# The modulation of the MLP half, summed between GLA's tasks in place of beside Hyena

## The chip, the cores and the metric

The program runs on one core of a Trainium2 chip, as one launch. A core has a matrix engine (TensorE, PE, with its weight loads shown as PEld), a vector engine (DVE), a scalar engine (ACT), GpSimd (POOL), a queue that issues most loads (SP) and 16 DMA engines. Each engine takes its instructions strictly in the order in which they were laid down when the program was built, and waits on semaphores for the others. The metric is the device time of an execution in microseconds; shorter is better.

## The reference

Two parts follow one another on one sequence of 1024 tokens of width 1024, with 256 context tokens, all in float32. The change lies in the first part, one block:

```python
silu_c = jax.nn.silu(c)
sh1, sc1, g1, sh2, sc2, g2 = jnp.split((silu_c @ w_mod[l] + b_mod[l])[:, None, :], N_MOD, axis=-1)
h = modulate(x, norm1_g[l], sh1, sc1)
...
y, yc = mixer(h, hc, rows, with_ctx_out, w_in[l], w_out[l], ...)   # [Hyena | GLA | GatedDeltaNet] @ w_out
x = x + g1 * y
x = x + g2 * sq_relu_mlp(modulate(x, norm2_g[l], sh2, sc2), w_mlp1[l], w_mlp2[l])
```

Of the six vectors of modulation, g1 is needed at the out-projection, sc2 and sh2 behind it, and g2 at the end of the MLP. Each is a row of 1024 numbers: the product of a vector of 1024 with a 1024 x 1024 part of w_mod. The second part, two layers of windowed attention and mLSTM, is not touched.

## The kernel before

The code emits instructions in the order of the Python program; a static scheduler then lays down the order of each engine by dependencies, buffers and its own estimates of durations. A buffer is a tile of a pool under a tag; a tag with two buffers lets two tiles take turns, and a load into a third waits until the last reader of the first is done. Matrix products in float32 are made of three products of high and low halves, so a weight tile is loaded raw, and split into hi (ACT) and lo (DVE or POOL).

Block 1 runs: modulation of the mixers' half, norm, in-projection, preparation of GDN (the gated delta net), then the scan of GDN in two lanes of two heads each, ten steps a head, then Hyena (two long convolutions by hand-written Fourier matrices, hy_mix and hy_conv), then GLA (gla_mix), then the out-projection (out_rows), and the MLP. The scheduler lets the scan run beside Hyena and GLA. The scan loads each head's k and q (L1275, L1276) and makes W in L1323.

The MLP half's four vectors come from mods1 (L1565), one block each in the order g1, sc2, sh2, g2. A block, mod_block (L371), has eight pieces: a load of 128 x 1024 of w_mod on SP into tile mr (L375, 512 KB, tag "wr" of two buffers), a scaling by the vector's entries on ACT (in place; the first piece writes the accumulator ma, tag "wh" of two buffers), and for the other seven a sum into ma on POOL (L387). Then eight matmuls with a column of ones sum ma over partitions, and DVE adds the bias. For g1 and g2 col_row turns the columns into a row in memory, by way of a small tile crow and a DMA on POOL's queue. That makes 32 loads, 32 scalings and 28 sums.

GLA goes through two head pairs p, each of two groups of tokens with levels of 64, 32, 16, 8, 4, 2, 1 and 0 tokens and an output; its products of decays with q and k are on POOL (eq and ek in L873, L874, and in L909 for the outputs), the exponentials on ACT, the differences on DVE (L867 to L870). A hook, step(p, i), is called between its tasks, 20 times for each p. At p = 1, i = 8 it loads g1 as a broadcast row and emits the eight tiles of w_out (wo_tile, L1556): a load into tag "wr", a multiplication by g1 on POOL (L1561), then hi and lo. At i = 12 and 14 the first half of GLA's rows is normalized. The results of the mixers go through memory, tensor yT, from which the out-projection loads tiles, also in tag "wr" (L1533), and splits them into ch (ACT) and cl (POOL).

PSUM has eight banks. The scan keeps three, mods1 has a pool of one and Hyena one of four.

Of the kernel before, what the change touches and what calls it, by code (L numbers as in the profile page):

```python
# [9 lines left out]
F32 = mybir.dt.float32  # L10
# [9 lines left out]
D = 1024  # L20
# [146 lines left out]
class Builder:  # L167
# [226 lines left out]
            nc.vector.tensor_add(out=outs[v], in0=p[:, v * 8 : v * 8 + 8], in1=b)  # L394
        yield

    def col_row(self, name, col):

        p = self.ps()
        self.tp(p[:8, :128], col)  # L400
        t = self.small([8, 128], "crow", 2)
        self.nc.vector.tensor_copy(out=t, in_=p[:8, :128])
        row = self.dram(name, [1, D])
        self.nc.gpsimd.dma_start(out=row[0].rearrange("(j p) -> j p", p=128), in_=t)
        return row
# [1156 lines left out]
        self.split(raw, hi, lo, leng=leng)  # L1562
        return hi, lo

    def mods1(self, tl):  # L1565

        A, c = self.A, self.sc["cc"][:, :, 0]
        m = {}
        for j, nm in ((2, "g1"), (4, "sc2"), (3, "sh2"), (5, "g2")):
            t = self.const(nm, [128, 8])  # L1570
            for _ in self.mod_block(tl, A["w_mod"][0][:, j * D : j * D + D], self.c["b_mod"][:, j * 8 : j * 8 + 8], [c], [t], "pool"):
                pass
            m[nm] = self.col_row(nm + "row", t) if nm[0] == "g" else t
        m["gs2"] = self.gs_cols("gs2", m["sc2"], self.c["norm2_g"])
        return m

    def mods2(self, tl, md):

# [130 lines left out]
    def block1(self, x3, ey):  # L1709
# [16 lines left out]
        with ExitStack() as e1:  # L1726
# [9 lines left out]
            with ExitStack() as e2:  # L1736
# [13 lines left out]
                tl = lambda tag, bufs, shape=(128, TT), dt=F32: self.tiler(pools[tag])(tag, bufs, shape, dt)  # L1750
# [34 lines left out]
            egg.close()  # L1785
            with ExitStack() as es:
                ep = ExitStack()
                ep.enter_context(self.psums(px=1))
                pmod = self.pools
                ep.enter_context(self.psums(px=4))  # L1790
                with ExitStack() as eh:
                    hl = self.tiler(self.pool(eh, "hym"))
                    ml = lambda tag, bufs, shape: self.wp.tile(list(shape), F32, name=self.nm(tag), tag={"mr": "wr", "ma0": "wh"}[tag], bufs=2)
                    eh.enter_context(self.smalls())
                    self.hy_mix(F, dr["hy"], yT, hl)
                    pmix, self.pools = self.pools, pmod
                    m = self.mods1(ml)
                    self.pools = pmix
                ep.close()
                es.enter_context(self.psums(pq=2, px=3))  # L1800

                eq, eA, eB = (ExitStack() for _ in range(3))
                with right():
                    eq.enter_context(self.psums(pm=3))
                    pm = self.pools["pm"]
                    eB.enter_context(self.smalls())
                    ol, lB, lA = (self.tiler(self.pool(e, n)) for e, n in ((eB, "o1"), (eB, "o1b"), (eA, "o1a")))
                wo = {}
                rows = lambda u, t: u[t * 128 : t * 128 + 128, :]
                KO = (0, 1, 5, 6, 7, 2, 3, 4)  # L1810
                hn = [None, None]
                op = self.pool(es, "orl")
                orows = op.tile([128, 8, 384], F32, name="orowsl")
                norm = lambda g: self.head_norm_out(orows, self.c["gla_ng"], dr["gla_gate"], yT, 256, self.tiler(op), self.ps, (g,))

                def step(p, i):
                    if p == 1:
                        if i == 8:
                            g1 = self.row_bc(self.wp.tile([128, D], F32, name="g1", tag="wh", bufs=2), m["g1"])
                            for k in KO:  # L1820
                                wo[k] = self.wo_tile(lA if k in (0, 1, 5, 6, 7) else lB, self.A["w_out"][0], k, gate=g1)
                        if i == 12:
                            hn[0] = norm(0)
                            next(hn[0])
                        if i == 14:
                            for _ in hn[0]:
                                pass

                with self.smalls():
                    self.gla_mix(sub("gla_"), orows, step)  # L1830
                hn[1] = norm(1)
                for _ in hn[1]:
                    pass
# [642 lines left out]
```

## Time and profile before

| | |
|---|---|
| median of three runs | 3687.88 us (3683.22 to 3688.8) |
| profiled execution | 3682.15 us |
| its span | 3680.4 us |
| PE, DVE, ACT, POOL busy | 3336.0, 2266.0, 1523.4, 1331.9 us |

The profile is of one execution. Busy time is the sum of an engine's instructions; the time of the profiled execution has 1.75 us around the span. Stretches are named by their time from the start of the span: GDN's preparation ends and Hyena's first convolution runs at about 758 to 841 us, Hyena ends at about 929, GLA's first pair runs from about 960 to 1073 and its second to about 1199, where the main block of the out-projection starts.

### The profile page before, as it was taken

The page shows a single profiled execution, that of the slowest core. Times are in us where ns is not written, and L with a number is a line of the kernel's source. Part 1 is how long each engine was busy: PE and PEld are TensorE (multiplying, and loading weights), DVE is VectorE, ACT ScalarE, POOL GpSimd, SP SyncE. Part 2 cuts the span into 40 slices and gives each one's busy share as a digit, 9 for nine tenths or more (in the row PEclk, how much of TensorE's full clock was granted, in tenths as well). Part 3 has the DMA queues.
Part 4 walks back from the last instruction along what each step waited for, and adds up shares of the span by engine and source line. Part 5 has one row for each costly group of instructions (what it writes and reads, how often), then busy time and mean ns, then how long its engine had stood idle before and what let it go on. Part 6 is the DMA issues. An engine that isn't in the chain of part 4 may idle for free.

```text
span 3680.4 us, 53188 instructions
## 1 busy us (share of the span) xinstructions
PE 3336.0 (91%) x19802; PEld 2775.0 (75%) x19802; DVE 2266.0 (62%) x4418; ACT 1523.4 (41%) x2967; POOL 1331.9 (36%) x1162
## 2 busy tenths in 40 slices
PE   7999989768896999999999699998899999998997
PEld 5668867656775778877788588887788778876885
DVE  8783642467568365555544756665677757665776
ACT  4443345431333442222211544443565554444662
POOL 2343432564547243333412201112545501113554
PEclk9899988777655999999999899999999999998998
DMA  5433543563313352222221211112544511124444
GB/s 201 145 118 100 142 130 107 192 203 114 94 46 101 121 183 92 74 72 74 90 81 46 70 50 52 51 51 87 152 121 126 170 57 55 55 70 130 121 132 140
DMA packets 346222, 388.03 MB, mean 105 GB/s; under 512 B 58099, under 2 KB 282787, under 8 KB 345964
## 3 DMA queue, kind: packets, MB, share of 16 engines
q1 hardware_dynamic: 322380, 300.33, 27.8%
q0 software_dynamic: 23584, 84.31, 6.3%
q8 instruction: 157, 2.57, 0.3%
q14 instruction: 101, 0.83, 0.1%
HBM read 296.07 MB, written 88.49 MB: 104 GB/s over the span
## 4 chain that ended last, share of the span: by engine, by line
PE 60%; DVE 15%; issue 7%; DMA 6%; ACT 5%; POOL 4%; SPq 1%; POOLq 0%; ACTq 0%; DVEq 0%
PE pm L256 34%; PE px L256 20%; PE pa L256 2%; PE px L265 2%; PE po L256 1%; DVE ma L271 1%; PE pa L265 1%; DMA mr<-in_w_ada 1%; DMA mr<-in_w_mod 1%; DVE ac L271 1%; POOL ma L387 1%; ACT e L268 1%; ACT mr L268 1%; DVE e L287 1%; DVE x L287 1%
## 5 line engine op out<-in xcount | busy, mean ns | idle before, releaser
L256 PE MATMUL pm<-x,wh 128*128 128x512 f32 (+3 forms) x4768 | 1430.2, 381 | 1.8 <-DVE x L287 1.8
L256 PEld LDWEIGHTS pm<-x,wh 128*128 128x128 f32 (+2 forms) x4768 | 863.9, 189 | 165.1 <-issue 8.4
L256 PE MATMUL pm<-x,wl 128*128 128x512 f32 (+3 forms) x2384 | 908.5, 381 | 26.5 <-ACT u L268 19.1
L256 PEld LDWEIGHTS pm<-x,wl 128*128 128x128 f32 (+2 forms) x2384 | 450.3, 189 | 110.6 <-ACT u L268 20.3
L256 PE MATMUL pm<-wo,ch 128*128 128x512 f32 x832 | 271.0, 407 | 0.0
L287 DVE TENSOR_TENSOR wl<-wr,wh 128x1024 fp32r<-128x1024 f32 (+1 forms) x110 | 144.0, 1309 | 170.2 <-ACT wh L268 169.8
L1652 DVE TENSOR_TENSOR oa<-px,oa 128x512 f32<-128x512 f32 x240 | 162.1, 688 | 132.2 <-PE px L256 131.9
L387 POOL TENSOR_TENSOR ma<-ma,mr 128x1024 f32<-128x1024 f32 x63 | 157.3, 2497 | 171.8 <-ACT mr L268 138.0
L268 ACT ACTIVATE u<-pm 128x512 f32<-128x512 f32 (+2 forms) x204 | 108.7, 544 | 261.3 <-PE pm L256 228.1
L256 PE MATMUL px<-w2h,ml 128*128 128x512 f32 x480 | 194.8, 406 | 19.8 <-DVE ml L287 10.1
L256 PE MATMUL px<-w2h,mh 128*128 128x512 f32 x480 | 192.3, 401 | 0.0
L256 PE MATMUL px<-w2l,mh 128*128 128x512 f32 x480 | 191.9, 400 | 0.0
L256 PEld LDWEIGHTS pm<-wo,ch 128*128 128x128 f32 x832 | 161.9, 196 | 32.8
L256 PE MATMUL pm<-wo,cl 128*128 128x512 f32 x416 | 171.1, 411 | 12.8 <-POOL cl L287 9.7
L275 POOL TENSOR_SCALAR mkw<-kr,gws 128x128 f32<-128x128 f32 x144 | 77.7, 543 | 282.0 <-PE px L256 240.2
L268 ACT ACTIVATE wh<-wr 128x1024 fp32r<-128x1024 f32 (+2 forms) x138 | 143.3, 1038 | 27.2 <-PE pm L256 15.4
L2360 DVE TENSOR_REDUCE amx<-pa 128x1 f32<-128x640 f32 (+2 forms) x144 | 107.3, 745 | 73.9 <-PE pa L256 72.8
L268 ACT ACTIVATE e<-e 128x1280 f32<-128x1280 f32 (+3 forms) x126 | 134.0, 1066 | 42.2 <-DVE e L275 38.7
L268 ACT ACTIVATE P<-pa,amx 128x640 f32<-128x640 f32 (+2 forms) x144 | 105.6, 733 | 95.3 <-DVE amx L275 83.9
L268 ACT ACTIVATE w2h<-wr 128x1024 fp32r<-128x1024 f32 x32 | 33.9, 1059 | 265.3 <-PE px L256 226.2
L268 ACT ACTIVATE mr<-mr,silu_cc 128x1024 f32<-128x1024 f32 x63 | 72.3, 1149 | 141.0 <-DVE ma L271 92.0
L1550 POOL TENSOR_TENSOR xr<-or,xr 128x512 f32<-128x512 f32 x72 | 93.3, 1296 | 98.0 <-DVE or L1549 80.9
(895 smaller groups left out, 7137.6 us busy)
## 6 DMA issues: line engine op xcount, KB each, us to landing
wr<-in_w_in SPq DMA_DIRECT2D x102, 512.0 KB
wr<-in_w_mlp SPq DMA_DIRECT2D x64, 512.0 KB
mr<-in_w_ada SPq DMA_DIRECT2D x48, 512.0 KB
mr<-in_w_mod SPq DMA_DIRECT2D x32, 512.0 KB
wr<-in_w_out SPq DMA_DIRECT2D x24, 512.0 KB
TF<-in_dft SPq DMA_DIRECT2D x54, 192.0 KB
rb<-npd SPq DMA_DIRECT2D x16, 640.0 KB
wr<-qd SPq DMA_DIRECT2D x36, 256.0 KB
```

Of the source, the lines that this page charges most:

```text
L256: self.nc.tensor.matmul(out, a, b, start=start, stop=stop)
L265: self.nc.tensor.transpose(out, in_, self.ident[:p, :p])
L268: self.nc.scalar.activation(out, in_, f, **kw)
L271: self.nc.vector.scalar_tensor_tensor(out=out, in0=in0, scalar=scalar, in1=in1, op0=op0, op1=op1)
L275: (eng or self.nc.vector).tensor_scalar(out=out, in0=in0, scalar1=s1, scalar2=s2, op0=op0, **kw)
L287: (leng or self.nc.vector).tensor_sub(out=lo, in0=src, in1=hi.bitcast(F32))
L387: nc.gpsimd.tensor_add(out=acc[v], in0=acc[v], in1=raw)
L1550: nc.gpsimd.tensor_add(out=xr[:, fs], in0=r, in1=xr[:, fs])
L1652: V.tensor_add(out=oa[t][:, fs], in0=p, in1=oa[t][:, fs])
L2360: V.reduce_max(m_, s[:, w0:768], axis=AX.X)
```

## The change

mods1 becomes a generator that yields after each piece and at the end of each block. The hook step takes one item of it at each of its 40 calls, and what is left is taken behind gla_mix. Its matmuls and transposes use GLA's banks. The two small tiles crow of g1 and g2 now lie in the pool of weights under the tag "wl", two buffers that the tiles of normalized rows (hng) also use. Hyena gets one pool of five banks.

```diff
--- before.py
+++ after.py
@@ -394,11 +394,12 @@
             nc.vector.tensor_add(out=outs[v], in0=p[:, v * 8 : v * 8 + 8], in1=b)
         yield
 
-    def col_row(self, name, col):
+    def col_row(self, name, col, t=None):
 
         p = self.ps()
         self.tp(p[:8, :128], col)
-        t = self.small([8, 128], "crow", 2)
+        if t is None:
+            t = self.small([8, 128], "crow", 2)
         self.nc.vector.tensor_copy(out=t, in_=p[:8, :128])
         row = self.dram(name, [1, D])
         self.nc.gpsimd.dma_start(out=row[0].rearrange("(j p) -> j p", p=128), in_=t)
@@ -1562,17 +1563,14 @@
         self.split(raw, hi, lo, leng=leng)
         return hi, lo
 
-    def mods1(self, tl):
+    def mods1(self, tl, m):
 
         A, c = self.A, self.sc["cc"][:, :, 0]
-        m = {}
         for j, nm in ((2, "g1"), (4, "sc2"), (3, "sh2"), (5, "g2")):
             t = self.const(nm, [128, 8])
-            for _ in self.mod_block(tl, A["w_mod"][0][:, j * D : j * D + D], self.c["b_mod"][:, j * 8 : j * 8 + 8], [c], [t], "pool"):
-                pass
-            m[nm] = self.col_row(nm + "row", t) if nm[0] == "g" else t
+            yield from self.mod_block(tl, A["w_mod"][0][:, j * D : j * D + D], self.c["b_mod"][:, j * 8 : j * 8 + 8], [c], [t], "pool")
+            m[nm] = self.col_row(nm + "row", t, self.wp.tile([128, D], F32, name="crow", tag="wl", bufs=2)[:8, :128]) if nm[0] == "g" else t
         m["gs2"] = self.gs_cols("gs2", m["sc2"], self.c["norm2_g"])
-        return m
 
     def mods2(self, tl, md):
 
@@ -1785,17 +1783,11 @@
             egg.close()
             with ExitStack() as es:
                 ep = ExitStack()
-                ep.enter_context(self.psums(px=1))
-                pmod = self.pools
-                ep.enter_context(self.psums(px=4))
+                ep.enter_context(self.psums(px=5))
                 with ExitStack() as eh:
                     hl = self.tiler(self.pool(eh, "hym"))
-                    ml = lambda tag, bufs, shape: self.wp.tile(list(shape), F32, name=self.nm(tag), tag={"mr": "wr", "ma0": "wh"}[tag], bufs=2)
                     eh.enter_context(self.smalls())
                     self.hy_mix(F, dr["hy"], yT, hl)
-                    pmix, self.pools = self.pools, pmod
-                    m = self.mods1(ml)
-                    self.pools = pmix
                 ep.close()
                 es.enter_context(self.psums(pq=2, px=3))
 
@@ -1808,12 +1800,15 @@
                 wo = {}
                 rows = lambda u, t: u[t * 128 : t * 128 + 128, :]
                 KO = (0, 1, 5, 6, 7, 2, 3, 4)
-                hn = [None, None]
+                hn, m = [None, None], {}
+                ml = lambda tag, bufs, shape: self.wp.tile(list(shape), F32, name=self.nm(tag), tag={"mr": "wr", "ma0": "wh"}[tag], bufs=2)
+                mods = self.mods1(ml, m)
                 op = self.pool(es, "orl")
                 orows = op.tile([128, 8, 384], F32, name="orowsl")
                 norm = lambda g: self.head_norm_out(orows, self.c["gla_ng"], dr["gla_gate"], yT, 256, self.tiler(op), self.ps, (g,))
 
                 def step(p, i):
+                    next(mods, None)
                     if p == 1:
                         if i == 8:
                             g1 = self.row_bc(self.wp.tile([128, D], F32, name="g1", tag="wh", bufs=2), m["g1"])
@@ -1828,6 +1823,8 @@
 
                 with self.smalls():
                     self.gla_mix(sub("gla_"), orows, step)
+                    for _ in mods:
+                        pass
                 hn[1] = norm(1)
                 for _ in hn[1]:
                     pass
```

The scheduler lays down the following. On ACT, at the end of Hyena's first convolution and of GDN's preparation (mr is a piece of modulation, W, G and rv are results of the preparation, P and Y are Hyena's), before:

```order
L268 ACTIVATE mr_8601<-mr_8601,silu_cc 128x1024
L268 ACTIVATE Y_8104<-EO_7891 128x256 x2
L268 ACTIVATE W_4927<-px_5296 128x480
L268 ACTIVATE mr_8605<-mr_8605,silu_cc 128x1024
L268 ACTIVATE W_4927<-px_5303 128x480
L268 ACTIVATE G_5311<-px_5312 96x512
L268 ACTIVATE mr_8609<-mr_8609,silu_cc 128x1024
L268 ACTIVATE G_5311<-px_5318 96x512
L268 ACTIVATE G_5311<-px_5324 96x256
L268 ACTIVATE mr_8613<-mr_8613,silu_cc 128x1024
L268 ACTIVATE rv_4883<-px_5329 128x480
L268 ACTIVATE mr_8617<-mr_8617,silu_cc 128x1024
```

and now:

```order
L268 ACTIVATE Y_8101<-EO_7888 128x256 x2
L268 ACTIVATE mr_9278<-mr_9278,silu_cc 128x1024
L268 ACTIVATE W_4927<-px_5303 128x480
L268 ACTIVATE G_5311<-px_5312 96x512
L268 ACTIVATE G_5311<-px_5318 96x512
L268 ACTIVATE G_5311<-px_5324 96x256
L268 ACTIVATE rv_4883<-px_5329 128x480
L268 ACTIVATE rv_4883<-px_5336 128x480
L268 ACTIVATE G_5344<-px_5345 96x512
```

One scaling stays among these rows, where there were six; of the 32 loads, 18 (blocks g1 and sc2) stay ahead of them.

On POOL, in the second group of GLA's first head pair, with block sh2 (ma, mr), now:

```order
L875 TENSOR_TENSOR ek_8966<-ek_8966,k_8530 128x512
L387 TENSOR_TENSOR ma_1718_9246<-ma_1718_9246,mr_9278 128x1024
L387 TENSOR_TENSOR ma_1718_9246<-ma_1718_9246,mr_9338 128x1024
L387 TENSOR_TENSOR ma_1718_9246<-ma_1718_9246,mr_9372 128x1024
L874 TENSOR_TENSOR eq_8965<-eq_8965,q_8529 128x512
L387 TENSOR_TENSOR ma_1718_9246<-ma_1718_9246,mr_9424 128x1024
L387 TENSOR_TENSOR ma_1718_9246<-ma_1718_9246,mr_9478 128x1024
L387 TENSOR_TENSOR ma_1718_9246<-ma_1718_9246,mr_9534 128x1024
L387 TENSOR_TENSOR ma_1718_9246<-ma_1718_9246,mr_9580 128x1024
L874 TENSOR_TENSOR eq_9007<-eq_9007,q_8529 128x512
L875 TENSOR_TENSOR ek_9008<-ek_9008,k_8530 128x512
```

Before, this place held GLA's products alone. Of w_out's eight products (L1561) two stood beside Hyena, and the rest in GLA's second pair; these rows are from its first group:

```order
L1561 TENSOR_TENSOR wr_9747<-wr_9747,g_9731 128x1024
L874 TENSOR_TENSOR ek_9506<-ek_9506,k_9372 128x512
L873 TENSOR_TENSOR eq_9555<-eq_9555,q_9371 128x512
L1561 TENSOR_TENSOR wr_9754<-wr_9754,g_9731 128x1024
L874 TENSOR_TENSOR ek_9556<-ek_9556,k_9372 128x512
L873 TENSOR_TENSOR eq_9607<-eq_9607,q_9371 128x512
L874 TENSOR_TENSOR ek_9608<-ek_9608,k_9372 128x512
L1561 TENSOR_TENSOR wr_9761<-wr_9761,g_9731 128x1024
L1561 TENSOR_TENSOR wr_9768<-wr_9768,g_9731 128x1024
L873 TENSOR_TENSOR eq_9649<-eq_9649,q_9371 128x512
```

Seven sums of a block stand now in the first pair with one GLA product between them, and all eight of w_out's products, line 1562 now, stand behind the second pair's first L909 (line 910 now).

At the end of GLA, on SP, from the loads of GLA's second pair to the out-projection (wr is a raw tile of w_out or of yT), before:

```order
L790 DMA v_9381<-gla_v 128x10x192
L1559 DMA wr_9747<-in_w_out 128x1024
L1559 DMA wr_9754<-in_w_out 128x1024
L1559 DMA wr_9761<-in_w_out 128x1024
L1559 DMA wr_9768<-in_w_out 128x1024
L1559 DMA wr_9775<-in_w_out 128x1024
L1559 DMA wr_9782<-in_w_out 128x1024
L1533 DMA wr_10271<-yT 128x2x128
```

and now, from the fourth of six loads of w_out:

```order
L1560 DMA wr_9722<-in_w_out 128x1024
L1560 DMA wr_9729<-in_w_out 128x1024
L1560 DMA wr_9736<-in_w_out 128x1024
L375 DMA mr_9765<-in_w_mod 128x1024
L375 DMA mr_9807<-in_w_mod 128x1024
L375 DMA mr_9839<-in_w_mod 128x1024
L375 DMA mr_9885<-in_w_mod 128x1024
L375 DMA mr_9981<-in_w_mod 128x1024
L375 DMA mr_10007<-in_w_mod 128x1024
L1534 DMA wr_10267<-yT 128x2x128 x2
L1534 DMA wr_10274<-yT 128x128
L1534 DMA wr_10274<-yT 128x3x128
```

The last six pieces of w_mod (g2) stand between w_out's loads and the first tile of yT; they were all ahead of GLA.

There, on PE, at the first matmuls of the out-projection (pm; px and pq are GLA's, and px from consts and ma is the column sum of g2), before:

```order
L256 MATMUL pq_9859<-eq_9811,ek_9812 32x32
L256 MATMUL pq_9860<-eq_9811,ek_9812 32x32
L256 MATMUL pm_10287<-wo_1805_9734,cl_10273 128x512
L256 MATMUL pm_10287<-wo_1806_9735,ch_10272 128x512
L256 MATMUL pm_10287<-wo_1805_9734,ch_10272 128x512
L256 MATMUL pm_10287<-wo_1808_9741,cl_10273 128x512
```

and now, where six rows like the two ahead are left out:

```order
L256 MATMUL px_10045<-eq_9935,ek_9936 128x128 x4
L256 MATMUL px_10046<-eq_9935,ek_9936 128x128 x4
L256 MATMUL px_10057<-consts,ma_1786_9659 128x1 x8
L256 MATMUL px_10069<-eq_9985,ek_9986 128x128
L256 MATMUL px_10070<-eq_9985,ek_9986 128x128
...
L256 MATMUL pm_10283<-wo_1794_9688,cl_10269 128x512
L256 MATMUL pm_10283<-wo_1795_9689,ch_10268 128x512
L256 MATMUL pm_10283<-wo_1794_9688,ch_10268 128x512
```

Of the out-projection, 24 matmuls stood before GLA's last levels; now none do, and g2's column sum stands ahead of the first.

## Rows read from the trace of the kernel before

**Rows 1.** The page, busy time by engine: us, share of span, instructions.
```profile
PE 3336.0 (91%) x19802; PEld 2775.0 (75%) x19802; DVE 2266.0 (62%) x4418; ACT 1523.4 (41%) x2967; POOL 1331.9 (36%) x1162
```

**Rows 2.** Windows: length; PE, PEld, DVE, ACT, POOL busy us; clock; DMA share; GB/s.
```profile
758.00:802.00 44.00, 27.59 (x166) 22.45 (x164) 30.34 (x44) 19.12 (x29) 25.15 (x16) 0.84 0.77 248
802.00:841.00 39.00, 22.17 (x100) 19.84 (x101) 28.32 (x31) 10.04 (x15) 30.60 (x14) 0.54 0.44 126
841.00:929.00 88.00, 78.82 (x426) 66.32 (x425) 60.91 (x137) 19.85 (x45) 38.07 (x17) 0.82 0.40 115
960.00:1073.00 113.00, 105.67 (x896) 92.40 (x895) 69.96 (x159) 35.69 (x70) 55.16 (x42) 0.61 0.15 42
1073.00:1139.00 66.00, 46.55 (x413) 38.34 (x412) 43.73 (x69) 27.52 (x91) 46.65 (x29) 0.55 0.22 68
1139.00:1199.00 60.00, 43.36 (x346) 35.83 (x346) 42.42 (x58) 20.98 (x60) 37.58 (x33) 0.59 0.34 110
```

**Rows 3.** Groups, 758 to 850 us: busy us, mean ns | idle before, releaser.
```profile
L387 POOL TENSOR_TENSOR ma<-ma,mr 128x1024 f32<-128x1024 f32 x13 | 31.8, 2447 | 17.8 <-ACT mr L268 17.8
L268 ACT ACTIVATE mr<-mr,silu_cc 128x1024 f32<-128x1024 f32 x12 | 13.8, 1146 | 29.9 <-DMA mr<-in_w_mod 29.9
...
L256 PE MATMUL px<-consts,ma 128*128 128x1 f32 x32 | 3.9, 249 | 1.4 <-POOL ma L387 1.4
```

**Rows 4.** Timeline of PE: start, us, instruction, count [idle before, releaser].
```profile
801.90 1.83 PE L265 MATMUL px<-consts,k 96*128 96x96 f32 x10 [14.86 <-DMA k<-gdn_k]
...
820.60 2.08 PE L256 MATMUL px<-st,k 96*128 96x128 f32 x8 [7.15 <-ACT at L268]
```

**Rows 5.** Timeline of SP, which issues loads, from 793 us.
```profile
793.54 0.33 SPq L375 DMA_DIRECT2D mr<-in_w_mod  x1
793.96 0.38 SPq L1275 DMA_DIRECT2D k<-gdn_k  x1
```

**Rows 6.** Waits of SP's queue, 758 to 850 us: total us, times, longest.
```profile
SPq L375 <- POOL ma L387: 24.0, 8, 5.1
```

**Rows 7.** Timeline of ACT: first and last of ten scalings, one later.
```profile
759.76 1.15 ACT L268 ACTIVATE mr<-mr,silu_cc 128x1024 f32<-128x1024 f32 x1 [1.21 <-DMA mr<-in_w_mod]
...
799.90 1.15 ACT L268 ACTIVATE mr<-mr,silu_cc 128x1024 f32<-128x1024 f32 x1 [2.42 <-DMA mr<-in_w_mod]
...
818.92 1.15 ACT L268 ACTIVATE mr<-mr,silu_cc 128x1024 f32<-128x1024 f32 x1 [7.57 <-DMA mr<-in_w_mod]
```

**Rows 8.** Three DVE lines: ns min/median/max, first and last start.
```profile
L698 DVE TENSOR_TENSOR t<-t,t x18: 406/424/3425, 697.5 to 890.7; 128x256 f32<-128x256 f32 x18
...
L867 DVE TENSOR_TENSOR eq<-b x28: 399/426/2249, 945.1 to 1181.4; 128x256 f32<-128x256 f32 x28
...
L1323 DVE TENSOR_TENSOR W<-px,W x36: 341/352/358, 830.2 to 1094.1; 128x192 f32<-128x192 f32 x36
```

**Rows 9.** Timeline of POOL in GLA's second head pair.
```profile
1106.29 2.34 POOL L1561 TENSOR_TENSOR wr<-wr,g 128x1024 f32<-128x1024 f32 x1 [2.10 <-DMA wr<-in_w_out]
...
1119.73 4.75 POOL L1561 TENSOR_TENSOR wr<-wr,g 128x1024 f32<-128x1024 f32 x2
...
1129.49 7.30 POOL L941 TENSOR_TENSOR orowsd<-orowsd,hnr 128x384 f32<-128x384 f32 x8
...
1139.07 1.45 POOL L909 TENSOR_TENSOR ek<-ek,q 128x512 f32<-128x512 f32 x1
```

**Rows 10.** Timeline of SP: six w_out loads from issue of first to last.
```profile
1100.39 31.36 SPq L1559 DMA_DIRECT2D wr<-in_w_out  x6
```

**Rows 11.** Timeline of PE: out-projection, the work after its first part, main block.
```profile
1167.61 0.76 PE L256 MATMUL pm<-wo,cl 128*128 128x512 f32 x1 [3.06 <-DVE hng L271]
...
1176.02 0.76 PE L256 MATMUL pq<-eq,ek 48*32 48x32 f32 x64
...
1198.80 0.79 PE L256 MATMUL pm<-wo,cl 128*128 128x512 f32 x1 [4.36 <-POOL cl L287]
```

**Rows 12.** DMA issues, 700 to 860 us: KB each, median us to landing.
```profile
g1row<-crow POOLq DMA_DIRECT2D x1, 4.0 KB, 4.0
```

## Prediction

> **What bounds the kernel now.** First the shares: the matrix engine PE is busy 91% of the span, VectorE (DVE) 62%, ScalarE (ACT) 41%, GpSimd (POOL) 36% [rows 1]. Over the whole kernel PE is the bound, and the change neither adds nor removes PE work, so it can only touch stretches where PE stands still. The windows around the change say where those are [rows 2]. From 758 to 841 us (the end of the in-projection's GDN preparation and the first half of Hyena) PE works 27.59 of 44 and 22.17 of 39 us; from 841 to 929 (the rest of Hyena, with scan steps of GDN) 78.82 of 88; in the first head pair of GLA (960 to 1073) 105.67 of 113; in the second pair 46.55 of 66 and 43.36 of 60. So Hyena's first half and GLA's second pair have idle PE, and GLA's first pair hardly any.
>
> Then, for 758 to 850 us, who fills and who waits. ACT scaled 12 modulation pieces and sat idle 29.9 us just before them for their loads; POOL did 13 sums of 2.447 us and sat 17.8 us before them for ACT [rows 3]. The engines run in order, so work placed behind such a piece waits with it. PE shows two such waits: 14.86 us until GDN's first k tile had landed, 7.15 us until an ACT copy into at [rows 4]. The k load was issued at 793.96, directly behind a modulation load at 793.54 [rows 5], and SP waited 24.0 us in eight places with such a load until a POOL sum had freed its buffer [rows 6]. The at copy stood behind a scaling that had waited 7.57 us for its load [rows 7].
>
> **The change part by part.**
>
> *Before 758 us.* In the order that is built, 18 of the 32 modulation loads (blocks g1 and sc2), and their sums on POOL, stay beside Hyena at the places they had up to about 758 us, so I cost that part at nothing. 14 loads and 14 sums (sh2 and g2) leave; one of their loads and its scaling stay in Hyena, and its sum waits until GLA. The fifth PSUM bank of Hyena is the one that the modulation had: it lets PE run one result further ahead of the engines that empty the banks. No row shows a wait for a bank by itself; I put it at nothing, and its other end, PE's 14.86 us idle in [rows 4], lies inside Hyena's bounds below.
>
> *Hyena, 758 to 929.* Three things fall away. The k wait: the load no longer queues behind modulation loads; of 14.86 us I take 12, since it needs its own flight. The wait for at: of 7.15 I take 5. The 32 modulation column sums on PE with the wait for the last POOL sum, 3.9 + 1.4 us, of which I take 3, since PE idles nearby anyway. Sum −20. What hides the rest: DVE is busy 28.32 of 39 and 60.91 of 88 us there, and three more scan steps are placed into Hyena. Lower bound −5 (the scan takes the room), upper −40 (the 22.0 of both waits, 5.3 of sums, and a third of the 14 × 2.447 = 34.3 us of POOL work that held others up).
>
> *GLA, first pair.* Here stand seven of the moved sums, six of them nearly together on POOL with only one GLA product between them. Before, a piece came every 4.46 us: ten scalings from 759.76 to 799.90 are nine intervals in 40.14 us [rows 7], two buffers taking turns. Six pieces so take 6 × 4.46 = 26.8 us, during which ACT and POOL do little for GLA. The last scan steps and the products with the 64 and 32 wide blocks cover part on PE; I take half as exposed: +12 (rounded down). Bounds: +30 if all of it and one wait more is exposed, −12 if the three scan steps that left this stretch (at some 4 us each, an estimate from the 264 us of its 36 W sums between 830.2 and 1094.1 [rows 8], 7.3 each, of which PE's share is part) count and the pieces hide.
>
> *GLA, second pair, first half (1073 to 1139).* Before, POOL gated four w_out tiles here at about 2.4 us each (2.34, and two in 4.75), and normalized GDN's rows in 7.30 us [rows 9]: 16.8 of its 46.65 us in 66. Both leave: the gatings now stand behind the first L909 product, GDN's normalization ahead of the pair. The scan itself, whose last W sum was at 1094.1 [rows 8], 21 us into this pair, now ends in the first pair. I take −20 (16.8 and part of the scan); bounds −5 (GLA's own chain ACT, POOL, PE holds it) and −30. The g1 row now goes out behind GDN's last normalized tile, since they share two buffers; its flight was 4.0 us [rows 12] and is covered unless GDN is late.
>
> *The end of GLA up to the out-projection.* Before, from L909's product at 1139.07 [rows 9] to the out-projection's main block at 1198.80 were 59.7 us, and 24 of its matmuls had run early, 1167.61 to 1176.02, 8.4 us [rows 11]. Now SP's queue holds, behind the g1 row, six w_out loads, then the six last g2 loads, then the yT tiles; all in the same two buffers. Six w_out loads took 31.36 us before [rows 10]; six pieces 26.8 us; yT's landing and its hi and lo parts some 6 (an estimate from the 4.0 us flight and 2 us of ACT and POOL). Sum 64, and about 2 behind L909: 66 against 59.7, and the 24 matmuls are no longer done ahead: +6 + 8 = +14. PE's queue has the g2 column sum just ahead of the first out-projection matmul, so PE can't start without it. Bounds: +5 (loads land faster while nothing else loads: DMA share 0.34) and +36 (pieces also wait behind GLA's products).
>
> *Sum.* −20 + 12 − 20 + 14 = −14. The sum is made against the profiled execution, 3682.15 us, span 3680.4: 3668. The median of the runs shown, 3687.88, lies 5.7 above, which gives 3674; I say 3672. The bounds together are −40 − 12 − 30 + 5 = −77 and −5 + 30 − 5 + 36 = +56; the four parts are unlikely to fall to one side all at once.
>
> **A rule weighed.** The row: L698, a DVE product of two SBUF tiles beside Hyena, took 424 ns at the median and 3425 at the most, and L867, the like in GLA, 426 and 2249 [rows 8]: a DVE instruction can be held for about one POOL sum. The Trainium skill, "SBUF — State Buffer", section "SBUF: two separate sides", says that DVE and GpSimd lock a shared port for a whole instruction, and a DVE instruction with two SBUF inputs is blocked by a GpSimd one that reads SBUF; the rows agree with it. By that rule the 34.3 us of moved sums hold DVE's GLA products just as they held Hyena's, and the Hyena term comes back in GLA.
>
> **The rivals.**
> *No change (3686).* The Hyena gain of 20 is given back by DVE and POOL in GLA: the same 34.3 us of sums beside DVE products of two tiles, L698's maximum for L867's. For: [rows 8]; DVE 69.96 of 113 busy. Against: L698 lost about 3.0 us at most per hit, and few of 18 hit; GLA's first pair waits for PE. The two parts that gain, −20 − 20, then meet +26 in GLA (three quarters of 34.3) and +14 in the tail: 0, so 3682 to 3688, and I say 3686.
> *Slower (3700).* The moved pieces stop GLA: in order on ACT and POOL, each of the 14 waits for its load as in Hyena, where 12 waited 29.9 us, 2.5 each, and POOL's sum adds 2.45. 14 × 4.95 = 69 exposed in the first pair and the tail, against −40 for Hyena and the second pair's first half and some 12 hidden: +17, 3699 to 3705. It decides when more than about 40 of these 69 us are exposed. For: the tail is one chain through two buffers with PE's queue behind it. Against: ACT is busy 20.98 and POOL 37.58 of 60 there, so there is room.
> *Larger gain (3643).* TensorE's granted clock, 0.61 in GLA's first pair against 0.82 in Hyena's second half [rows 2] (means over stretches at 1.2 and 2.4 GHz), rises there: 105.67 × (1 − 0.61/0.82) = 27 us less. For: PE-bound stretch. Against: nothing in the change makes PE denser for certain, and more waits make it thinner.
>
> **How the numbers follow.** Forecast (−8 to −30) 0.42, larger gain 0.06, no change 0.20, slower 0.32. A measurement of this kernel can tell 0.2%, 7.4 us, from no change; so faster 0.48, same 0.20, slower 0.32. The range 3640 to 3712 reaches over the larger gain and most of the slower case; below it stay about 0.05, above about 0.12. The likeliest case alone has 3654 to 3680.
>
> **What would show it.** Right: PE's wait for k under 4 us, Hyena's last output at about 909 instead of 929; about 34 us of modulation sums in GLA; the stretch from the first L909 of the second pair to the out-projection's main block some 66 to 75 us. Wrong: waits of PE in GLA's first pair that lead to a modulation piece and sum to more than 25 us; POOL standing at GDN's normalization before the second pair for over 20 us, since then the scan has not come forward; the chain to the out-projection over 90 us; Hyena ending at 925 or later.

## The result, and the profile after

The changed kernel took 3710.24 us (median of 4 runs, 3702.53 to 3716.26), the kernel before 3685.92 (3683.22 to 3688.8): a ratio of 1.0065, 95% interval 1.0044 to 1.0086. It became slower by 24 us. The profiled execution took 3716.26 us, its span is 3714.5. It is the slowest of its four, and the execution of the profile before, 3682.15 us, lies below all four that its median is made of; so the two profiles are 34 us apart, ten more than the medians.

First the windows, the same as in [rows 2] (length; PE, PEld, DVE, ACT, POOL busy; granted clock; DMA share; GB/s):

```profile
core 0: us, PE busy (x) PEld busy (x) DVE busy (x) ACT busy (x) POOL busy (x), PEclk, DMA share, GB/s
758.00:802.00 44.00, 32.34 (x174) 27.34 (x173) 27.47 (x46) 12.09 (x23) 18.20 (x12) 0.80 0.62 174
802.00:841.00 39.00, 33.59 (x161) 29.71 (x160) 28.13 (x49) 7.08 (x15) 19.19 (x8) 0.66 0.34 94
841.00:929.00 88.00, 74.38 (x450) 64.29 (x448) 54.97 (x124) 22.05 (x49) 35.09 (x19) 0.84 0.42 120
960.00:1073.00 113.00, 102.30 (x768) 89.88 (x769) 63.81 (x146) 42.80 (x121) 54.47 (x37) 0.50 0.23 69
1073.00:1139.00 66.00, 47.89 (x425) 39.89 (x423) 45.06 (x65) 19.15 (x31) 47.12 (x37) 0.55 0.33 111
1139.00:1199.00 60.00, 27.83 (x260) 22.23 (x260) 44.65 (x50) 24.86 (x62) 51.98 (x30) 0.50 0.30 101
```

From 802 to 841 us PE now works 33.59 of 39, where it worked 22.17; so Hyena's first half was filled, as meant. From 1139 to 1199 it works only 27.83 of 60, where it worked 43.36. The wait for the first k tile answers to [rows 4]; it fell from 14.86 to 5.97 us, and the scan starts 23 us earlier (timeline of PE). The wait for at, 7.15 us, has no row any more.

```profile
778.47 1.83 PE L265 MATMUL px<-consts,k 96*128 96x96 f32 x10 [5.97 <-DMA k<-gdn_k]
```

To say where time came from and went, four landmarks are used, all on POOL's timeline: the write of Hyena's last output (yT from EO), the clearing of k for GLA's second pair, the second pair's first output product (L909 before, L910 now) and the first write of x behind the out-projection. They tell how far POOL's queue has come; what the other engines have done by then can differ. Before, with the product at 1139.07 in [rows 9]:

```profile
929.49 0.59 POOL L1516 DMA_DIRECT2D yT<-EO  x1
...
1069.90 2.37 POOL L787 MEMSET k<- 32x1280 f32 x2 [4.59 <-PE px L256]
...
1219.20 0.58 POOL L1843 DMA_DIRECT2D x<-xr  x1 [15.46 <-DVE xr L1546]
```

And after, with the first two gatings by g1 and the first and the last of the six sums of g2 among them:

```profile
913.04 0.55 POOL L1517 DMA_DIRECT2D yT<-EO  x1 [0.40 <-ACT EO L268]
...
1084.29 2.37 POOL L788 MEMSET k<- 32x1280 f32 x2
...
1126.01 1.26 POOL L910 TENSOR_TENSOR ek<-ek,q 128x512 f32<-128x512 f32 x1 [1.34 <-ACT ek L268]
1132.01 4.84 POOL L1562 TENSOR_TENSOR wr<-wr,g 128x1024 f32<-128x1024 f32 x2 [4.74 <-DMA g<-g1row]
...
1185.84 3.34 POOL L387 TENSOR_TENSOR ma<-ma,mr 128x1024 f32<-128x1024 f32 x1
...
1208.09 2.34 POOL L387 TENSOR_TENSOR ma<-ma,mr 128x1024 f32<-128x1024 f32 x1 [1.36 <-ACT mr L268]
...
1246.80 0.59 POOL L1840 DMA_DIRECT2D x<-xr  x1 [17.05 <-DVE xr L1547]
```

Hyena ends 16.4 us earlier. From there to the second pair it takes 171.3 us in place of 140.4 (+30.8); from there to its first output product 41.7 in place of 69.2 (−27.5); up to here 13.1 us are gained. From there to the first write of x it takes 120.8 in place of 80.1 (+40.7). At that write the kernel is 27.6 us late, at the last of the eight 27.1. The rest of the span, 2374.6 us before and 2381.7 after, is the same program. In the runs below it has 2376 to 2389 us (2397 in sum_late, which moves a step into it), so 7 us there are no more than what executions differ by.

The last stretch, read on three engines. SP's queue, from the load of g1's row (the duration of several is from the issue of the first to that of the last):

```profile
1128.19 0.32 SPq L1520 DMA_DIRECT2D g<-g1row  x1
1139.38 30.60 SPq L1560 DMA_DIRECT2D wr<-in_w_out  x6
1173.19 29.94 SPq L375 DMA_DIRECT2D mr<-in_w_mod  x6
1206.76 5.79 SPq L1534 DMA_DIRECT2D wr<-yT  x6
```

PE around the out-projection's first matmuls (answers to [rows 11]), and its largest waits from 1139 to 1250:

```profile
1210.48 3.57 PE L256 MATMUL px<-consts,ma 128*128 128x1 f32 x16 [19.72 <-POOL ma L387]
1213.98 2.08 PE L256 MATMUL px<-eq,ek 48*128 48x128 f32 x16
1215.99 0.79 PE L256 MATMUL pm<-wo,cl 128*128 128x512 f32 x1
...
1218.51 0.39 PE L256 MATMUL pm<-wo,cl 128*128 128x512 f32 x1
```

```profile
PE px L256 <- POOL ma L387: 19.7, 1, 19.7
PE px L265 <- POOL orowsl L942: 10.2, 1, 10.2
```

One sees six loads of w_out, then six pieces of w_mod, then the first tiles of yT, one after another; and PE standing 19.72 us at g2's column sum, with products of GLA behind it that do not need this sum.

### The profile page after: what moved, and what is told of

The parts are those of the page before. It is cut to its first block, busy times and chain, and to the rows that moved or that the text cites. A ratio compares the mean times of both kernels' runs of the same rounds, so it can differ in the third digit from the quotient of the medians.

```text
span 3714.5 us, 53196 instructions
## 1 busy us (share of the span) xinstructions
PE 3347.1 (90%) x19802; PEld 2786.5 (75%) x19802; DVE 2269.3 (61%) x4418; ACT 1524.4 (41%) x2967; POOL 1327.1 (36%) x1162
## 4 chain that ended last, share of the span: by engine, by line
PE 60%; DVE 14%; issue 8%; DMA 6%; ACT 5%; POOL 4%; SPq 1%; POOLq 0%; ACTq 0%; DVEq 0%
PE pm L256 34%; PE px L256 20%; PE pa L256 2%; PE px L265 2%; PE po L256 1%; PE pa L265 1%; DVE ma L271 1%; DMA mr<-in_w_ada 1%; DVE ac L271 1%; POOL ma L387 1%; ACT e L268 1%; ACT mr L268 1%; DVE x L287 1%; DVE wl L287 1%; POOL cl L287 1%
## 5 line engine op out<-in xcount | busy, mean ns | idle before, releaser
L256 PE MATMUL pm<-x,wl 128*128 128x512 f32 (+3 forms) x2384 | 909.8, 382 | 26.8 <-ACT u L268 19.2
L268 ACT ACTIVATE wh<-wr 128x1024 fp32r<-128x1024 f32 (+2 forms) x138 | 143.3, 1038 | 27.5 <-PE pm L256 15.0
L2357 DVE TENSOR_REDUCE amx<-pa 128x1 f32<-128x640 f32 (+2 forms) x144 | 107.4, 746 | 74.2 <-PE pa L256 73.3
L256 PEld LDWEIGHTS px<-w2h,ml 128*128 128x128 f32 x480 | 93.0, 194 | 48.0 <-DVE ml L287 18.0
```

The lines of the kernel that those rows point to most:

```text
L256: self.nc.tensor.matmul(out, a, b, start=start, stop=stop)
L268: self.nc.scalar.activation(out, in_, f, **kw)
L2357: V.reduce_max(m_, s[:, w0:768], axis=AX.X)
```

## The experiments

Theory T: the loss is made at the end of GLA, by the six last pieces between w_out's loads and yT's, and by their column sum in PE's queue. Rivals: P, the loss is made in the first pair, by the pieces there; S, POOL's sums hold DVE's instructions on two SBUF tiles wherever they stand. Ratios are to the kernel before on the same chip, with the 95% interval; the stretches between the four landmarks are from one profile each, in us. How far one profile can be trusted is told by four_banks: it has the changed kernel's order on ACT, DVE and POOL, and on PE but for four matmuls, and its stretches differ from the changed kernel's by up to 6.1 us.

| kernel | ratio | Hyena's end | to 2nd pair's k | to its output product | to first write of x |
|---|---|---|---|---|---|
| before | 1 | 929.5 | 140.4 | 69.2 | 80.1 |
| changed | 1.0065 (1.0044 to 1.0086) | 913.0 | 171.3 | 41.7 | 120.8 |
| no_g2 | 0.9983 (0.9963 to 1.0003) | 911.9 | 162.9 | 46.4 | 85.2 |
| neither | 0.9985 (0.9966 to 1.0004) | 909.7 | 166.8 | 48.4 | 88.2 |
| all_in_pair1 | 1.0031 (1.0012 to 1.0050) | 918.7 | 176.0 | 53.8 | 87.1 |
| banks_only | 1.0077 (1.0052 to 1.0103) | 916.1 | 213.4 | 37.8 | 81.0 |
| sum_late | 1.0037 (1.0021 to 1.0054) | 911.9 | 172.3 | 43.1 | 106.2 |
| g2_late | 1.0020 (1.0006 to 1.0034) | 911.8 | 171.9 | 53.5 | 88.4 |
| g1_first | 1.0005 (0.9990 to 1.0019) | 916.4 | 168.7 | 57.4 | 82.6 |
| four_banks | 1.0069 (1.0048 to 1.0090) | 912.4 | 165.2 | 42.6 | 121.2 |
| mods_first | 1.0099 (1.0075 to 1.0122) | 1012.6 | 129.9 | 36.8 | 79.2 |

### Without g2's block

```diff
 for j, nm in ((2, "g1"), (4, "sc2"), (3, "sh2"), (5, "g2")):
+    if nm == "g2":
+        m["g2"] = m["g1"]
+        continue
```

> The changed kernel with the fourth block (g2: eight loads, scalings, seven sums) left out; the g1 row stands in for g2, so the MLP's gate is not computed. Theory T (the end of GLA): the six last pieces, behind w_out's loads in two buffers, with their column sum ahead of GLA's last levels on PE, cost some 30 us between the second pair's first output product and the out-projection; so 3710 - 30 = 3680, PE's 19.7 us wait for the last sum is gone, and that stretch is back at 60 to 66 us. Rival P (the first pair: what the third block's seven pieces and the scan do there costs more than all else): only two pieces leave the first pair here, so 3700 to 3706. Rival S (POOL's sums hold DVE's products): seven sums of 28 leave, about half of the loss, 3695 to 3700.

Measured: 0.9983, which is 30 us (0.82%) below the changed kernel. In the profiles the first write of x comes 40.4 us earlier, 35.6 of them in the last stretch (85.2 for 120.8). Two landmarks on POOL, and PE's largest waits from 1121 to 1250, where the column sum's is gone:

```profile
1121.22 1.26 POOL L910 TENSOR_TENSOR ek<-ek,q 128x512 f32<-128x512 f32 x1
...
1206.43 0.58 POOL L1843 DMA_DIRECT2D x<-xr  x1
```

```profile
PE px L256 <- DVE at L902: 10.1, 4, 5.7
PE px L265 <- POOL orowsl L942: 3.7, 2, 3.4
```

That is T in place and size: it expected 3680, P and S 3695 or more, and the median was 3683.51, with before at 3687.91 on that chip. T's 60 to 66 us from the output product to the main block were not reached; the main block starts at 1195.37, 74.2 us behind the product:

```profile
1195.37 0.79 PE L256 MATMUL pm<-wo,cl 128*128 128x512 f32 x1
```

The run takes away one more link, which T does not name. The tile for g1's row lies in tag "wh", two buffers, behind the accumulators of sh2 and g2. So in the changed kernel its load waits until PE's column sum of sh2 has read its accumulator, 10.9 us on SP's queue. SP's wait, which the profile puts down to the instruction right behind that sum, at 1128.02, and then the sum on PE:

```profile
SPq L1520 <- PE px L265: 10.9, 1, 10.9
```

```profile
1124.59 3.57 PE L256 MATMUL px<-consts,ma 128*128 128x1 f32 x16
```

Without g2 the tile takes the buffer of sc2, whose sum is long done: the load goes out at 1108.12 in place of 1128.19, and w_out's first product comes at 1112.09, ahead of the output product, in place of 1132.01, behind it. No run separates this wait from the six loads.

### Without sh2's block too

```diff
+    if nm in ("sh2", "g2"):
+        m[nm] = m["sc2" if nm == "sh2" else "g1"]
+        continue
```

> The changed kernel with the third and fourth block (sh2, g2) left out, sc2 and the g1 row in their place, so the MLP's shift and gate are not computed; no modulation piece is left in GLA. What it is below the run without g2 alone is the price of the seven sh2 pieces in the first pair. T: 5 to 12 us less than without g2, 3668 to 3675. P: 25 us less or more, 3675 to 3680, with the first pair about 26 us shorter than in the changed kernel. S: about as much less again as the first step, 3683.

Measured: 0.9985, beside 0.9983 without g2 alone; the medians, 3679.46 and 3683.51, are 4 us apart, which these intervals do not tell from nothing. T had expected 5 to 12 us for the seven sums in the first pair, P 25 or more (its 3675 to 3680 holds the median, but as a step down from 3700 to 3706), S a step as large as the first. The first pair is 4.5 us shorter than in the changed kernel, not 26: P falls. It shows two further things. The first pair's stretch is 166.8 us with no piece in GLA at all, where it was 140.4. And with all 14 late pieces gone the kernel is faster by only 0.15%, in an interval that reaches past 1: with this order of the rest, moving them had hardly more than that to gain.

### All late pieces in the first pair

```diff
-                    next(mods, None)
+                    if p == 0:
+                        next(mods, None)
+                        next(mods, None)
```

> The changed kernel with two pieces for each of the hook's 20 calls of the first pair, none in the second, so all 14 late pieces stand ahead of w_out's loads; all work is done. T: the end of GLA goes back to about 60 us and the first pair grows by the six pieces' 27 us of loads, part hidden: 3680 to 3692. P: the first pair takes all of the growth and more, 3715 to 3730. S: the same number of POOL sums stands beside DVE's products in GLA, so no change from 3710.

Measured: 1.0031. The last stretch came back to 87.1 us, and the first pair with the half behind it took 16.8 us more than in the changed kernel (176.0 + 53.8 against 171.3 + 41.7), with six of w_out's eight gatings ahead of the output product again. The median, 3701.39, lies between T's range and P's, and below S's 3710.

### Only the banks

```diff
-                ep.enter_context(self.psums(px=1))
-                pmod = self.pools
-                ep.enter_context(self.psums(px=4))
+                ep.enter_context(self.psums(px=5))
...
-                    pmix, self.pools = self.pools, pmod
                     m = self.mods1(ml)
-                    self.pools = pmix
```

> The kernel before with only the banks changed: Hyena has a pool of five, and the modulation, called where it was, takes its tiles from it. The scheduler then puts the last 14 sums between Hyena's last output and GLA's first products. T and P: what Hyena gained of 16 us is given back by 14 sums of 2.4 us in a row on POOL ahead of GLA, 3686 to 3700. If the fifth bank is worth something by itself, or the place beside Hyena was the only harm, below 3675.

Measured: 1.0077, slower than expected (3717.23 against 3686 to 3700). POOL's timeline, with Hyena's last output, the first and the last of the 14 sums, and GLA's first product:

```profile
916.06 0.55 POOL L1516 DMA_DIRECT2D yT<-EO  x1 [0.40 <-ACT EO L268]
918.95 2.35 POOL L387 TENSOR_TENSOR ma<-ma,mr 128x1024 f32<-128x1024 f32 x1 [2.34 <-ACT ma L268]
...
977.96 2.34 POOL L387 TENSOR_TENSOR ma<-ma,mr 128x1024 f32<-128x1024 f32 x1 [2.33 <-ACT mr L268]
...
1021.85 1.26 POOL L873 TENSOR_TENSOR eq<-eq,q 128x512 f32<-128x512 f32 x1
```

Hyena ends 13.4 us ahead of before, nearly as early as in the changed kernel; but GLA's first product stands behind the 14 sums and comes at 1021.85, where it came at 960.30 before. Of these 61.6 us part is made good: the first write of x is 29.1 us late. What leaves Hyena has to be hidden elsewhere.

### Only the last step of g2 late

```diff
-                    next(mods, None)
+                    if p == 0 or i < 15:
+                        next(mods)
...
-                    for _ in mods:
-                        pass
...
         for _ in self.out_rows(...):
             pass
+        for _ in mods:
+            pass
```

(The columns gs2 are made behind sc2 here, since they are needed earlier.)

> The changed kernel with only the last step of g2 (column sum on PE, bias, transpose, row) taken behind the out-projection; its eight loads, scalings and seven sums stay where they are. It splits the 40 us that the end of GLA lost without the pieces (85 us from the second pair's first output product to the first write of x without g2, 121 with it). If PE's queue is what costs (GLA's last levels held behind the column sum), GLA's last matmuls run in PE's 19.7 us wait: 15 to 20 us back, 3690 to 3695. If the loads are what costs (yT's tiles behind six pieces in two buffers), the main block still starts about 1211: at most 6 us back, 3704 to 3710.

Measured: 1.0037, 0.28% (10 us) below the changed kernel, in intervals that overlap a little; the median, 3700.7, lies between the two ranges. PE did GLA's last products in the former wait, yet the main block still starts at 1215.59; the first write of x follows it after 17.9 us, where it took 30.8. PE's timeline, then POOL's:

```profile
1196.46 3.09 PE L256 MATMUL px<-eq,k 48*128 48x128 f32 x16 [0.25 <-ACT eq L268]
...
1215.59 0.80 PE L256 MATMUL pm<-wo,cl 128*128 128x512 f32 x1 [0.19 <-POOL cl L287]
```

```profile
1233.50 0.54 POOL L1840 DMA_DIRECT2D x<-xr  x1
```

So both reasons hold, each for a part: PE's queue for the 12.9 us between 30.8 and 17.9, and the chain of loads for the start of the main block, which did not move. That chain has the 10.9 us wait for g1's tile here too.

### g2 between the pieces of the out-projection

```diff
+                    if p == 0 and i < 17:
+                        next(mods)
...
+                    for _ in range(10):
+                        next(mods)
                     self.gla_mix(sub("gla_"), orows, step)
...
         for _ in self.out_rows(...):
-            pass
+            next(mods, None)
```

> The changed kernel with g1's block taken whole ahead of GLA, sh2's in the first pair, and g2's block between the pieces of the out-projection, behind the first tile of yT; all work is done. If the end of GLA lost its 30 us to the pieces and sum that stand ahead of the out-projection, that stretch comes back to 80 to 90 us and the whole to 3680 to 3690. If pieces cost the same wherever yT's tiles take turns with them in two buffers, it stays at 3700 to 3710.

Measured: 1.0020; the last stretch is back at 88.4 us, the median (3695.8) 6 us above the range. The scheduler puts g2's seven sums into GLA's second pair and behind it all the same, 1170.5 to 1213.3. But the load of g1's row goes out at 1110.20 and the first three of yT's from 1151.65, ahead of g2's, and g2's column sum stands at 1243.8, behind the out-projection's start. In this order the pieces do not hold it.

### g1 ahead of GLA

```diff
                 with self.smalls():
+                    for _ in range(10):
+                        next(mods)
                     self.gla_mix(sub("gla_"), orows, step)
```

> The changed kernel with ten items of the generator taken ahead of GLA (g1's block whole), the rest as it is, so that the scheduler has all 14 late sums in GLA's first pair and none at the end. If only the place at the end costs, the end comes back (80 to 90 us) and the first pair takes what it took with seven more sums before, 10 to 20 us: 3690 to 3702, near the run with all in the first pair. If the first pair hides them, as it hid the seven sh2 pieces (no difference between the runs without g2 and without both), 3680 to 3686.

Measured: 1.0005, no difference from before, and 0.6% below the changed kernel; the median, 3690.61, is at the lower edge of the first range. All 14 late sums stand in GLA's first pair here, as in all_in_pair1, and its stretch is no longer than in the changed kernel (168.7); the half behind it, with six gatings in it, is 15.7 us longer. From Hyena's end to the first write of x the run takes 308.7 us, where the changed kernel takes 333.8, all_in_pair1 316.9, neither 303.4 and before 289.7. The same number of sums beside DVE's differences, 0.6% apart: S falls. DVE's line 868 (867 before) shows that a difference can still be held, 1951 ns at the most:

```profile
L868 DVE TENSOR_TENSOR eq<-b x28: 403/428/1951, 940.0 to 1187.5; 128x256 f32<-128x256 f32 x28
```

### Hyena with four banks

```diff
-                ep.enter_context(self.psums(px=5))
+                ep.enter_context(self.psums(px=4))
```

> The changed kernel with Hyena's pool at four banks again; the scheduler lays down the same order on PE and POOL as with five. If Hyena's 16 us came from the pieces that left, its last output stays at 911 to 916 us and the whole at 3700 to 3710. If the fifth bank gave some of it, PE waits for banks in Hyena, and its last output comes 5 us or more later, 917 to 929.

Measured: 1.0069, as the changed kernel. Hyena's last output is written at 912.38 (913.04 in the changed kernel):

```profile
912.38 0.55 POOL L1517 DMA_DIRECT2D yT<-EO  x1 [0.40 <-ACT EO L268]
```

The fifth bank gave nothing that can be told.

### The modulation ahead of Hyena

```diff
+                    m = self.mods1(ml)
                     self.hy_mix(F, dr["hy"], yT, hl)
-                    m = self.mods1(ml)
```

(On the edit of banks_only.)

> The kernel before with the modulation called ahead of Hyena in place of behind it, its tiles in Hyena's pool of five: all 28 sums stand then ahead of Hyena's second half, and none in GLA. If only the place at the end of GLA is dear, the end keeps its 80 to 88 us. Pieces crowd the preparation of GDN and Hyena, so its last output comes 10 to 30 us later than 929; the two first w_out gatings leave GLA. 3685 to 3710; faster than 3680 only if Hyena hides the pieces, which its waits for them in the kernel before (29.9 us on ACT) speak against.

Measured: 1.0099, slower than all; the median, 3722.6, is above the range. Hyena ends 83 us later than before, not 10 to 30: the scheduler lets the whole of GDN's scan run ahead of Hyena's end, 36 steps of W in place of 15 (GDN's rows are normalized at 1024.52, 12 us behind Hyena's end, where it was 200 us before: 1129.49 against 929.49). The end of GLA, with no piece there, takes 79.2 us, just below the 80 to 88 that were expected.

## Why the prediction was wrong, by its own steps

**The direction was wrong**: −14 us was forecast, and +24 came. The step that failed is the end of GLA: put at +14, it measured +40.7, above its upper bound of +36. The time lies in the range, whose upper end, 3712, was there for the slower rival (3700). That rival is the case that came, though not as it was told: it spread the cost over the first pair and the end; the first pair with the half behind it has +3.3, and the end has the rest. Two of the signs that the prediction names show it: PE's wait for k is 5.97 us, not under 4, and the chain to the out-projection is 90.0, at the mark for wrong.

**Hyena** (−20): right. Measured −16.4, by the k wait (14.86 to 5.97) and the at wait (7.15, gone); four_banks shows that the pieces, and not the bank, were the reason.

**The first pair** (+12) **and the half behind it** (−20): +30.8 and −27.5, together +3.3 where −8 was forecast. The +12 was for the pieces, and the pieces are not what came: the first pair grew by 26.4 us with no piece in it (neither). Nor is it the scan: 18 of its 36 steps of W start in this stretch before, in the changed kernel and in neither, since three went ahead to Hyena and three came from the half behind. The windows from Hyena's last output to the second pair's k, in the order before, changed, neither (as in [rows 2]):

```profile
929.49:1069.90 140.41, 121.37 (x993) 106.31 (x992) 86.84 (x205) 41.69 (x84) 66.93 (x48) 0.62 0.27 72
```

```profile
913.04:1084.29 171.25, 142.56 (x1013) 125.20 (x1012) 95.95 (x218) 61.29 (x154) 93.76 (x62) 0.55 0.30 87
```

```profile
909.74:1076.53 166.79, 140.45 (x1004) 123.86 (x1003) 89.23 (x218) 51.33 (x144) 75.27 (x55) 0.56 0.21 57
```

In neither PE worked 19.1 us longer on nearly as many matmuls, and stood 7.3 us more. Its granted clock was 0.56 in place of 0.62; 121.37 × 0.62 / 0.56 = 134.4, so by this estimate 13 of the 19.1 us are the clock's. The sum had put the clock at nothing, and weighed it only as a gain. Why it was lower here no run shows.

The half behind fell by 20.8 us in neither, near the −20 of the forecast, and by 27.5 in the changed kernel. The scan has left it, and of w_out's products, of which five stood there before and not four (the fifth at 1136.75), two stand there in neither and none in the changed kernel. The last W was at 1094.1 [rows 8], in the changed kernel at 1043.5:

```profile
L1324 DVE TENSOR_TENSOR W<-px,W x36: 335/354/359, 796.6 to 1043.5; 128x192 f32<-128x192 f32 x36
```

**The end of GLA** (+14): the step that turned the sign. The mechanism was right, one chain of loads through two buffers; the size was not: +40.7. The two main terms were right: six w_out loads took 30.60 us (31.36 was used) and the six pieces 29.94 (26.8). What was left out is the rest of the chain, worked out from SP's rows above: from the output product at 1126.01 to the first of those six loads 13.4 us (2 were used), since the load of g1's row (1128.19, held by sh2's column sum; the forecast had the row as covered) and the gating and splitting of the first two tiles come ahead; between loads and pieces 3.2; between the pieces and yT 3.6; from yT's issue to the main block 9.2 (6 were used). 13.4 + 30.6 + 3.2 + 29.9 + 3.6 + 9.2 = 89.9, where 66 was forecast. POOL, which gates and sums for this chain, worked 70.79 us of it, where it worked 37.31 of 59.73 before; how much its pace adds to that of the loads no run shows. Behind the main block's start another 10.4 us went, about the 8 that were counted for the early matmuls; but sum_late shows that 12.9 came from GLA's own last products, which stood behind the column sum on PE. The prediction says of that sum only that the out-projection cannot start without it, and puts no price on GLA behind it.

**The rule that was weighed.** L698 and L867, which the prediction calls products, are differences of two SBUF tiles. The longest of L867's (now L868) in the changed kernel took 8.35 us, beside four of GLA's own POOL products in a row (1090.87 to 1099.06), with no modulation sum among them:

```profile
1091.00 8.35 DVE L868 TENSOR_TENSOR eq<-b 128x256 f32<-128x256 f32 x1 [1.14 <-PE px L256]
```

The Trainium skill, "SBUF — State Buffer", section "SBUF: two separate sides", has a DVE instruction with two SBUF inputs and a GpSimd one that reads SBUF exclude each other for a whole instruction; the row agrees with it. By that rule the moved sums would hold DVE's differences in GLA as in Hyena; g1_first, with all 14 of them there and no loss against before, shows that this did not set the time.

**The larger gain** by a higher clock did not come: the granted clock from 960 to 1073 was 0.50, where it had been 0.61. (3672 − 27 would have been 3645, not 3643.)

What stays open: why the clock was lower in the first pair; how the end's loss divides between the six pieces, the wait for g1's tile and POOL; and the rest of the span. In its profile no_g2 was 12.8 us ahead of before at the first write of x; its median keeps 4.4 of that (3683.51 against 3687.91), its ratio 6.3. The rest of the span differed by up to 14 us between profiles (22 with sum_late), and the profile before has the shortest; this is not taken apart.

## What to carry to other kernels

Work that is moved into a gap is to be priced in every in-order queue that it enters and in every buffer that it holds: here the pieces cost little beside GLA's first pair, and much in SP's queue ahead of yT and in PE's, where a small sum stood ahead of products that did not need it. Where transfers take turns in two buffers, count the chain from its first link, with the seams: two long terms that were right gave 66 us, the whole was 90. And before moving work, leave it out in a trial: without the 14 pieces the kernel was 0.15% faster, which, with the order that the scheduler gave the rest, left little for any place of theirs to bring.

## What the runs showed of the hardware

PE's clock was lower in most of GLA than before. In the changed kernel the granted clock was 0.50, the lower level of 1.2 GHz throughout, from 960 to 1073, where PE was busy 102.30 of 113 us, and again from 1139 to 1199, where it was busy 27.83 of 60. In the kernel before these two windows had 0.61 and 0.59 [rows 2]. The main block's first matmul of 512 columns took 0.79 us at 1215.99, another 0.39 at 1218.51, 2.5 us later, with the clock risen.

The clock also differs between kernels of nearly the same order: from Hyena's last output to the second pair's k it was 0.59 in four_banks and 0.55 in the changed kernel, and the stretch took 165.2 and 171.3 us.
